# Three attentions of a two-block model: score products over 128 rows instead of 128, 64 and 96

## The chip, the cores and the metric

The kernel runs on one core of a Trainium2 chip. The time is the device time of one execution in microseconds (us), the median of the runs of the same kernel. The engines of the core are TensorE (PE in the rows, its weight loads PEld), VectorE (DVE), ScalarE (ACT), GpSimd (POOL) and SyncE (SP), whose queue issues nearly all DMAs of this kernel. A product on TensorE takes two operands from on-chip memory (SBUF): one is loaded as weights, the other streams through, and both lie with the summed index on the partitions, which are called rows here. The result goes to a bank of PSUM, where several products can be added up.

## The reference

The reference computes, for one sequence of 512 tokens with 1024 features, two blocks in a row. The first has two layers: attention over chunks with a relative bias, then a feed forward with a causal convolution; latent attention, then the same feed forward. The second has a gated feed forward, a mixer (differential attention and a matrix memory side by side), and a gated feed forward. The three attentions are what is touched. Cut to their score products:

```python
# first layer, 16 heads of 64 (chunk_rel_attention)
s = jnp.einsum('bqhd,bkhd->bhqk', qc, kc).astype(jnp.float32) * scale + bias[None]
...
# second layer, 16 heads, 64 features and 32 rotary ones (mla_attention)
s = (jnp.einsum('bqhd,bkhd->bhqk', qn, k_nope).astype(jnp.float32)
     + jnp.einsum('bqhd,bkd->bhqk', qr, k_rope).astype(jnp.float32)) * scale
...
# second block, 8 heads of two parts of 64 (diff_attention)
s = jnp.einsum('bqhcd,bkhcd->bchqk', qi, k,
               preferred_element_type=jnp.float32) * scale
```

Each is followed by a mask, a softmax over the keys and the product with the values; the differential attention subtracts the second part's probabilities from the first's with a learnt weight before that.

## The kernel before, in words

Activations lie transposed: features on the 128 partitions, the 512 tokens as columns. Every matrix operand is kept as two numbers of TensorE's fp32r type, an upper part (the value rounded) and a lower part (what is left); a product of two such operands is three products on TensorE, upper by upper, upper by lower, lower by upper (`mm3`, L325 to L329). The lower by lower product is left out there.

A head has 64 features, so one operand of 128 rows can hold an upper part in one half and a lower part in the other. `stacked` (L521) makes that from the 128 rows of a pair of heads, rows 0 to 63 of the even head and 64 to 127 of the odd one. For the queries, operand e holds the upper part in rows 64 e on and the lower part in the other rows. For the keys, operand e holds the upper part in both halves. A third tile, `low`, holds the lower parts of both heads. The moves between halves of the partitions are DMAs, two for queries and two for keys, 64 rows by 512 columns each, issued by SP. `stacked_scores` (L536) then makes the scores of a query tile of 128 with the keys up to its end (128, 256, 384 or 512 columns) of two products: queries by doubled keys over 128 rows (upper by upper and lower by upper at once, L540), then the 64 rows of the upper queries by the 64 rows of the lower keys (L541). In the latent attention a third product on the same bank adds the rotary part (L903): 32 features, stacked in 96 rows as upper, lower, upper of the queries (`qr`) against upper, upper, lower of the keys (`kr`).

`heads` (L481) runs over the heads and, for each, over four query tiles: scores, softmax on VectorE and ScalarE (`softmax`, L471, with a bias tile `b` or a mask), then, two tiles behind, the transposes of the probabilities (`transpose`, L505) and after the fourth the product with the values (`values`, L513). The score banks `ps_s` are two. The weights are streamed: `wload` (L304) loads a tile `wr` and splits it into `wh` on ScalarE and `wl` on VectorE.

The three attentions differ in how far ahead keys and queries are made. In the first layer `project(p)` (L687) makes a pair's queries and keys while the odd head of the pair before it runs. In the latent attention (L866ff) a pair is made when the even head of the pair before it begins. In the differential attention (`project(hd)`, L1247) the two parts of one head take the places of the two heads of a pair, and a head is made when the one before it begins. In the first two, a pair's output goes to memory (`pair_out`) and all outputs are brought back after the heads by `pairs_back` (L557) into two buffers of the tag `tn`, which norms use for their temporaries too; the product with the output weights follows (`branch_out`, L726).

A tile scheduler sets the order of each engine's instructions: it takes the program in the order of the code and the readiness of tiles, and lets products of the next projection fill places in which TensorE would wait for the softmax. A tile of a tag waits until the oldest of the tag's buffers is free. SP's queue is worked off in order, and a DMA that has to wait holds what stands behind it.

## Time and profile before

| | us |
| --- | --- |
| times of three runs | 2762.89, 2767.37, 2770.97 |
| median | 2767.37 |
| span of the profiled execution | 2771.6 |
| TensorE busy | 2659.2 (96%) |
| TensorE's weight loads | 2129.6 (77%) |
| VectorE busy | 1759.9 (63%) |
| ScalarE busy | 1205.0 (43%) |
| GpSimd busy | 91.8 (3%) |

The profile is of one execution, whose span is 4.2 us over the median of the timed runs. Busy shares are means over stages with different limits, so the stages have to be read one by one. The score products of the first layer run from 90 to 252 us of the span, those of the latent attention from 770 to 905, those of the differential attention from 1762 to 1944. In the rows, matmuls overlap, since the next begins while the last one's results still drain: the length of one product is no measure of its pace, the distance of two starts is. L540 is line 540 of the kernel before; an entry such as `ps_s<-k,q` names the tile written and the tiles read, and `64*128 64x512` is a weight of 64 rows by 128 columns and a moving operand of 64 rows by 512 columns.

### The profile page before, as it was taken

To read this page: it belongs to the slowest core of one execution; us is meant where nothing else is said; L and a number is where in the kernel's file an instruction comes from. 1 tells how busy PE (TensorE), PEld (TensorE's weight loads), DVE (VectorE), ACT (ScalarE), POOL (GpSimd) and SP (SyncE) were. 2 spreads that over 40 slices of the span, in tenths; PEclk is the share of its full clock that TensorE was granted. 3 is DMA by queue.
4 is the path that set the end of the run, shared out by engine and by line. 5 is a ranking of instruction groups with operands and counts; after the bars stand their busy time and mean duration, and the time that the engine had idled before them with its cause. 6 is when DMAs were issued, how large, how long until landed. Compare 5 with 4: busy or idle time off the path is not lost.

```text
span 2771.6 us, 33871 instructions
## 1 busy us (share of the span) xinstructions
PE 2659.2 (96%) x12306; PEld 2129.6 (77%) x12306; DVE 1759.9 (63%) x3349; ACT 1205.0 (43%) x2100; POOL 91.8 (3%) x138
## 2 busy tenths in 40 slices
PE   7999899999899999999899999999999999999997
PEld 5777778788677778878788888777777777788886
DVE  7777896866778896966733335788456456533334
ACT  5565532334567442324522223566446334422222
POOL 1000200000000100000100001000000000100000
PEclk9999999999899999999999999999999999999999
DMA  8664476652143475753133332322247754233331
GB/s 271 188 184 144 145 248 204 223 173 79 43 106 111 139 229 187 252 176 120 54 99 93 98 113 80 92 75 78 72 149 258 239 186 133 77 95 95 99 107 46
DMA packets 138092, 385.24 MB, mean 139 GB/s; under 512 B 22322, under 2 KB 26546, under 8 KB 137924
## 3 DMA queue, kind: packets, MB, share of 16 engines
q1 hardware_dynamic: 137924, 383.06, 43.6%
q8 instruction: 98, 1.61, 0.2%
q14 instruction: 70, 0.57, 0.1%
HBM read 341.05 MB, written 26.21 MB: 133 GB/s over the span
## 4 chain that ended last, share of the span: by engine, by line
PE 33%; issue 13%; DVE 2%; DMA 1%; ACT 1%; POOL 1%; SPq 0%; DVEq 0%; ACTq 0%; POOLq 0%
PE ps_g L329 9%; PE ps_g L327 9%; PE ps_g L328 9%; PE ps_s L541 1%; DMA stg<-xc 1%; PE ps_t L327 1%; PE ps_t L328 1%; PE ps_t L329 1%; PE ps_s L540 0%; PE ps_o L367 0%; POOL ul L400 0%; PE ps_t L509 0%; POOL acc L361 0%; DMA mv<-mv 0%; DVE tn L393 0%
## 5 line engine op out<-in xcount | busy, mean ns | idle before, releaser
L327 PE MATMUL ps_g<-uh,wh 128*128 128x512 f32 (+1 forms) x2244 | 866.2, 389 | 30.7 <-ACT uh L340 11.7
L328 PE MATMUL ps_g<-ul,wh 128*128 128x512 f32 (+1 forms) x2244 | 875.7, 391 | 15.4 <-POOL ul L400 11.9
L329 PE MATMUL ps_g<-uh,wl 128*128 128x512 f32 (+1 forms) x2244 | 868.3, 388 | 1.1 <-DVE wl L311 1.1
L310 ACT CAST wh<-wr 128x1024 fp32r<-128x1024 f32 (+4 forms) x406 | 411.6, 1015 | 990.3 <-PE ps_g L328 730.6
L311 DVE TENSOR_TENSOR wl<-wr,wh 128x1024 fp32r<-128x1024 f32 (+4 forms) x406 | 479.1, 1181 | 284.7 <-ACT wh L310 270.4
L327 PEld LDWEIGHTS ps_g<-uh,wh 128*128 128x128 f32 x2244 | 425.3, 191 | 128.5 <-ACT uh L340 14.3
L328 PEld LDWEIGHTS ps_g<-ul,wh 128*128 128x128 f32 x2244 | 428.3, 191 | 111.5 <-POOL ul L400 20.3
L329 PEld LDWEIGHTS ps_g<-uh,wl 128*128 128x128 f32 x2244 | 428.7, 191 | 89.0 <-DVE wl L311 3.8
L461 DVE CUSTOM_DVE_ANT_0 wr<-wr,cact 128x1024 f32<-128x1024 f32 x184 | 225.8, 1232 | 73.0 <-DMA wr<-mod 72.9
L327 PE MATMUL ps_g<-hidh,wh 128*128 128x512 f32 x640 | 252.9, 395 | 7.8 <-ACT hidh L340 7.8
L329 PE MATMUL ps_g<-hidh,wl 128*128 128x512 f32 x640 | 253.0, 395 | 0.9 <-DVE wl L311 0.9
L328 PE MATMUL ps_g<-hidl,wh 128*128 128x512 f32 x640 | 252.9, 395 | 0.0
L327 PEld LDWEIGHTS ps_g<-hidh,wh 128*128 128x128 f32 x640 | 120.4, 188 | 37.9 <-ACT hidh L340 9.5
L329 PEld LDWEIGHTS ps_g<-hidh,wl 128*128 128x128 f32 x640 | 120.7, 189 | 29.7 <-DVE wl L311 1.3
L328 PEld LDWEIGHTS ps_g<-hidl,wh 128*128 128x128 f32 x640 | 120.7, 189 | 29.1 <-DVE hidl L341 0.6
L444 DVE SCALAR_TENSOR_TENSOR h<-ps_g,mods,h 128x512 f32<-128x512 f32 (+1 forms) x112 | 72.8, 652 | 94.1 <-PE ps_g L329 93.5
L444 DVE SCALAR_TENSOR_TENSOR h<-ps_g,hg,h 128x512 f32<-128x512 f32 (+1 forms) x64 | 43.6, 682 | 134.4 <-PE ps_g L329 134.2
L477 ACT ACTIVATE p<-p,st 128x128 f32<-128x128 f32 (+1 forms) x192 | 107.2, 560 | 30.2 <-DVE st L476 29.2
L929 DVE TENSOR_TENSOR cv<-ps_g,cv 128x512 f32<-128x512 f32 x44 | 30.4, 691 | 137.9 <-PE ps_g L329 137.2
L361 POOL TENSOR_TENSOR acc<-acc,sq 128x256 f32<-128x256 f32 x42 | 35.9, 855 | 2049.0 <-ACT sq L360 1365.7
L340 ACT CAST hidh<-cv 128x512 fp32r<-128x512 f32 x88 | 54.6, 621 | 93.8 <-DVE cv L756 93.8
L340 ACT CAST pth<-ps_t 128x128 fp32r<-128x128 f32 (+3 forms) x160 | 65.7, 424 | 53.7 <-PE ps_t L509 52.5
(362 smaller groups left out, 3607.7 us busy)
## 6 DMA issues: line engine op xcount, KB each, us to landing
wr<-mod SPq DMA_DIRECT2D x184, 512.0 KB, 4.2
wr<-fin SPq DMA_DIRECT2D x88, 512.0 KB, 4.4
wr<-fout SPq DMA_DIRECT2D x40, 512.0 KB, 3.9
wr<-w1g SPq DMA_DIRECT2D x22, 512.0 KB, 3.6
wr<-w1u SPq DMA_DIRECT2D x22, 512.0 KB, 3.6
wr<-w2g SPq DMA_DIRECT2D x22, 512.0 KB, 3.5
wr<-w2u SPq DMA_DIRECT2D x22, 512.0 KB, 3.5
wr<-w1d SPq DMA_DIRECT2D x20, 512.0 KB, 3.6
```

The source lines that it names most:

```text
L310: nc.scalar.copy(h[:, :n], r[:, :n])
L311: nc.vector.tensor_tensor(l[:, :n], r[:, :n], h[:, :n].bitcast(F32), ALU.subtract)
L327: mm(ps, wh, xh, start=start, stop=False)
L328: mm(ps, wh, xl, start=False, stop=False)
L329: mm(ps, wl, xh, start=False, stop=stop)
L340: self.nc.scalar.copy(h, src)
L361: (eng or nc.vector).tensor_tensor(acc[:, cs], acc[:, cs], s[:, cs], ALU.add)
L444: self.nc.vector.scalar_tensor_tensor(self.h[j][:, cs], ps, g, self.h[j][:, cs], ALU.mult, ALU.add)
L461: nc.vector.tensor_tensor_reduce(w, w, cact, 1.0, 0.0, ALU.mult, ALU.add, accum_out=self.mods[:, j:j + 1])
L477: nc.scalar.activation(p[:, :n], p[:, :n], AF.Exp, bias=st[:, 0:1], scale=-1.0, accum_out=st[:, 1:2])
L541: nc.tensor.matmul(s, q[rs, qs], low[rs, ks], start=False, stop=stop)
L929: nc.vector.tensor_tensor(t, pss[1], t, ALU.mult)
```

## The change

The keys' lower parts are doubled like their upper parts. A fourth tile `low1` (tag `tn`, two buffers) holds the odd head's lower parts in both halves; the third tile, once its upper rows have been moved to `low1`, gets the even head's lower parts in both. `stacked_scores` then uses all 128 rows for the second product as well: queries with upper and lower parts by the lower parts of the keys, so the lower by lower product is now computed too. The keys need five moves instead of two; the last one, `low[b]` from `low[a]`, overwrites rows that the second and the third read. In the latent attention the rotary queries are stacked in four blocks of 32 rows (upper, lower, upper, lower) with four moves a group instead of three, and the rotary keys fill 128 rows. The diff, without the removal of comments:

```diff
     def stacked(self, src, tiles, keys, scale=1.0):
         nc = self.nc
-        x, y, low = tiles
+        x, y, low = tiles[:3]
         a, b = slice(0, 64), slice(64, 128)
         nc.scalar.mul(x, src, scale)
         nc.vector.scalar_tensor_tensor(low, src, scale, x.bitcast(F32), ALU.mult, ALU.subtract)
         nc.scalar.mul(y[b], src[b], scale)
         move = lambda o, i: nc.sync.dma_start(o.bitcast(F32), i.bitcast(F32))
-        move(y[a], (x if keys else low)[b])
-        move(x[b], (x if keys else low)[a])
+        if keys:
+            low1 = tiles[3]
+            move(x[b], x[a])
+            move(low1[b], low[b])
+            move(low1[a], low[b])
+            move(y[a], y[b])
+            move(low[b], low[a])
+        else:
+            move(y[a], low[b])
+            move(x[b], low[a])

-    def stacked_scores(self, s, q, k, low, e, i, stop=True):
+    def stacked_scores(self, s, q, k, low, i, stop=True):
         nc = self.nc
-        rs, qs, ks = slice(64 * e, 64 * e + 64), slice(i * P, i * P + P), slice(0, i * P + P)
+        qs, ks = slice(i * P, i * P + P), slice(0, i * P + P)
         nc.tensor.matmul(s, q[:, qs], k[:, ks], start=True, stop=False)
-        nc.tensor.matmul(s, q[rs, qs], low[rs, ks], start=False, stop=stop)
+        nc.tensor.matmul(s, q[:, qs], low[:, ks], start=False, stop=stop)
...
                 k = [pa.tile([P, T], F32R, tag="k", bufs=6, name="k") for _ in range(3)]
+                k.append(self.tmp(dt=F32R, tag="tn", bufs=2))
...
-                    self.stacked_scores(s, q[e], k[e], k[2], e, i)
+                    self.stacked_scores(s, q[e], k[e], k[2 + e], i)
...
-            nc.scalar.copy(kr[0:96], t[0:96])
-            nc.vector.tensor_tensor(kr[64:96], t[64:96], kr[64:96].bitcast(F32), ALU.subtract)
+            nc.scalar.copy(kr, t)
+            nc.vector.tensor_tensor(kr[64:128], t[64:128], kr[64:128].bitcast(F32), ALU.subtract)
...
-                        for q, x in enumerate((h, l, h)):
+                        for q, x in enumerate((h, l, h, l)):
...
                 kn = [pm.tile([P, T], F32R, tag="k", bufs=6, name="kn") for _ in range(3)]
+                kn.append(self.tmp(dt=F32R, tag="tn", bufs=2))
...
-                    self.stacked_scores(s, qn[e], kn[e], kn[2], e, i, False)
-                    nc.tensor.matmul(s, qr[e][0:96, qs], kr[0:96, :n], start=False, stop=True)
+                    self.stacked_scores(s, qn[e], kn[e], kn[2 + e], i, False)
+                    nc.tensor.matmul(s, qr[e][:, qs], kr[:, :n], start=False, stop=True)
...
                 qk = [pd.tile([P, T], F32R, tag="qk", bufs=10, name="qk") for _ in range(5)]
+                qk.append(self.tmp(dt=F32R, tag="tn", bufs=2))
...
-                        self.stacked_scores(s, qk[c], qk[2 + c], qk[4], c, i)
+                        self.stacked_scores(s, qk[c], qk[2 + c], qk[4 + c], i)
```

The scheduler moves instructions with it. In the three listings before and after, numbers behind names tell buffers of one name apart.

TensorE, first layer, where the fifth head (the even head of the third pair) begins, before: `ps_s` are score banks, `k` and `q` keys and queries, `ps_g` the next pair's projection from the weights `wh` and `wl`, `ps_t` transposes of the probabilities `p`.

```order
L540 MATMUL ps_s_1416<-k_1253,q_1251 128x128
L541 MATMUL ps_s_1416<-k_1255,q_1251 128x128
L540 MATMUL ps_s_1431<-k_1253,q_1251 128x256
L541 MATMUL ps_s_1431<-k_1255,q_1251 128x256
L329 MATMUL ps_g_1512<-uh_122,wl_1296 128x512
L327 MATMUL ps_g_1512<-uh_124,wh_1295 128x512
L509 MATMUL ps_t_1425<-ident_67,p_1388 128x128 x3
L328 MATMUL ps_g_1512<-ul_125,wh_1295 128x512
```

And after, at the same place (between the two pieces, 10 more products of `ps_g` and 7 transposes):

```order
L509 MATMUL ps_t_1422<-ident_67,p_1373 128x128 x2
L549 MATMUL ps_s_1432<-k_1265,q_1263 128x128
L549 MATMUL ps_s_1447<-k_1265,q_1263 128x256
L327 MATMUL ps_g_1529<-uh_124,wh_1308 128x512
L328 MATMUL ps_g_1529<-ul_125,wh_1308 128x512
...
L328 MATMUL ps_g_1529<-ul_133,wh_1308 128x512
L329 MATMUL ps_g_1529<-uh_132,wl_1309 128x512
L327 MATMUL ps_o_1463<-pth_1352,vsh_1091 64x512
L327 MATMUL ps_g_1566<-uh_118,wh_1525 128x512
L550 MATMUL ps_s_1432<-k_1267,q_1263 128x128
L550 MATMUL ps_s_1447<-k_1267,q_1263 128x256
```

Before, the second score product stood right behind the first; after, the first products of both query tiles come ahead, then products of the next projection, and the second products of both tiles follow these.

SP's queue, first layer, the moves of the same pair's keys, with what each waits for in brackets, before: `b` is a bias tile, `wr` a weight or modulation tile, `tn<-oa1` a load of `pairs_back`.

```order
L532 DMA q_1251<-sq_1287 64x512 [waits DMAHW4_49,Activation_49]
L562 DMA tn_2630<-oa1_607 128x512 [waits DMAHW5_49,DMAHW1_49]
L532 DMA k_1254<-k_1253 64x512 [waits DMAHW6_49,Activation_49]
L460 DMA wr_1966<-mod 128x1024 [waits DMAHW7_49,DVE_49]
L532 DMA k_1253<-k_1253 64x512 [waits DMAHW6_49,DMAHW0_49,DVE_49]
L702 DMA b_1583<-bias 128x512 [waits DVE_49,Pool_49]
```

And after:

```order
L533 DMA k_1265<-k_1265 64x512 [waits DMAHW7_49,DVE_49]
L533 DMA tn_1268<-k_1267 64x512 [waits DMAHW0_49]
L533 DMA tn_1268<-k_1267 64x512 [waits DMAHW1_49]
L533 DMA k_1266<-k_1266 64x512 [waits DMAHW2_49,Activation_49]
L712 DMA b_1603<-bias 128x512 [waits DMAHW3_49,DVE_49,Pool_49]
L307 DMA wr_2031<-wqk 128x1024 [waits DMAHW4_49,DVE_49]
L533 DMA k_1267<-k_1267 64x512 [waits DMAHW5_49,DMAHW1_49,DMAHW0_49]
L307 DMA wr_2068<-wqk 128x1024 [waits DMAHW6_49,DVE_49]
```

The two moves of the keys became five, the last waits for the landings of the two into `tn` (DMAHW0 and DMAHW1), a weight load stands right behind it, and the load `tn<-oa1` has gone from this place to behind the heads.

TensorE, first layer, the last but two of the heads, query tiles two and three, before: `ps_g_2676` and `ps_g_2702` are products with the output weights, `ps_o` those with the values.

```order
L540 MATMUL ps_s_2347<-k_2004,q_2002 128x256
L541 MATMUL ps_s_2347<-k_2005,q_2002 128x256
L509 MATMUL ps_t_2356<-ident_67,p_2241 128x128 x4
L540 MATMUL ps_s_2378<-k_2004,q_2002 128x384
L541 MATMUL ps_s_2378<-k_2005,q_2002 128x384
L327 MATMUL ps_g_2676<-uh_2626,wh_2672 128x512
L328 MATMUL ps_g_2676<-ul_2627,wh_2672 128x512
L329 MATMUL ps_g_2676<-uh_2626,wl_2673 128x512
L327 MATMUL ps_o_2363<-pth_2164,vsh_2079 64x512
L327 MATMUL ps_g_2676<-uh_2632,wh_2672 128x512
L328 MATMUL ps_g_2676<-ul_2633,wh_2672 128x512
```

And after:

```order
L549 MATMUL ps_s_2379<-k_2028,q_2026 128x256
L550 MATMUL ps_s_2379<-tn_2030,q_2026 128x256
L509 MATMUL ps_t_2388<-ident_67,p_2269 128x128 x4
L549 MATMUL ps_s_2410<-k_2028,q_2026 128x384
L550 MATMUL ps_s_2410<-tn_2030,q_2026 128x384
L327 MATMUL ps_o_2395<-pth_2192,vsh_2107 64x512
L509 MATMUL ps_t_2419<-ident_67,p_2368 128x128
L549 MATMUL ps_s_2423<-k_2028,q_2026 128x512
```

The products with the output weights between the score products have gone from here; they stand behind the heads now.

## Rows read from the trace of the kernel before

**Rows 1.** The page: span, and each engine's busy time, share and instructions.
```profile
span 2771.6 us, 33871 instructions
...
PE 2659.2 (96%) x12306; PEld 2129.6 (77%) x12306; DVE 1759.9 (63%) x3349; ACT 1205.0 (43%) x2100; POOL 91.8 (3%) x138
```

**Rows 2.** Table by stretch: length, PE, PEld, DVE, ACT, POOL, PEclk, DMA share, GB/s.
```profile
90.00:262.00 172.00, 169.36 (x819) 122.91 (x820) 136.98 (x422) 108.83 (x263) 2.44 (x14) 0.99 0.56 169
770.00:906.00 136.00, 134.43 (x678) 96.06 (x677) 108.89 (x360) 96.26 (x251) 0.00 (x0) 0.95 0.38 105
1762.00:1945.00 183.00, 182.48 (x928) 141.59 (x927) 146.00 (x412) 121.61 (x280) 0.00 (x0) 1.00 0.28 78
```

**Rows 3.** TensorE's waits, 75 to 262 us: total, times, longest.
```profile
PE ps_s L540 <- DMA k<-k: 3.6, 1, 3.6
PE ps_s L540 <- DVE st L476: 1.5, 2, 1.2
```

**Rows 4.** TensorE's timeline in stage B: start, length, instruction.
```profile
809.01 0.39 PE L540 MATMUL ps_s<-kn,qn 128*128 128x512 f32 x1
809.33 0.49 PE L541 MATMUL ps_s<-kn,qn 64*128 64x512 f32 x1
809.75 0.50 PE L903 MATMUL ps_s<-kr,qr 96*128 96x512 f32 x1
810.09 0.39 PE L328 MATMUL ps_o<-ptl,vs 128*64 128x512 f32 x1
810.32 0.39 PE L329 MATMUL ps_o<-pth,vs 128*64 128x512 f32 x1
810.54 0.34 PE L327 MATMUL ps_o<-pth,vs 128*64 128x384 f32 x1
```

**Rows 5.** TensorE's timeline in stage A.
```profile
170.27 0.40 PE L540 MATMUL ps_s<-k,q 128*128 128x512 f32 x1
170.60 0.50 PE L541 MATMUL ps_s<-k,q 64*128 64x512 f32 x1
171.03 0.50 PE L329 MATMUL ps_g<-uh,wl 128*128 128x512 f32 x1
171.37 0.39 PE L328 MATMUL ps_o<-ptl,vsh 128*64 128x512 f32 x1
```

**Rows 6.** TensorE's timeline in stage C.
```profile
1821.92 0.50 PE L541 MATMUL ps_s<-qk 64*128 64x512 f32 x1
1822.35 0.50 PE L540 MATMUL ps_s<-qk 128*128 128x512 f32 x1
1822.78 0.50 PE L541 MATMUL ps_s<-qk 64*128 64x512 f32 x1
```

**Rows 7.** TensorE's timeline in the mixer, behind the differential attention.
```profile
2187.76 1.77 PE L1128 MATMUL ps_t<-slr 10*128 10x512 f32 x4
2189.46 0.50 PE L327 MATMUL ps_g<-uh,wh 128*128 128x512 f32 x1
2189.80 0.39 PE L328 MATMUL ps_g<-ul,wh 128*128 128x512 f32 x1
```

**Rows 8.** Instructions on ps_s: count, min/median/max ns, first and last start, forms.
```profile
L541 PE MATMUL ps_s<-k,q x64: 323/409/676, 90.5 to 251.5; 64*128 64x128 f32 x16, 64*128 64x256 f32 x16, 64*128 64x384 f32 x16, 64*128 64x512 f32 x16
```

**Rows 9.** DMA issues: count, KB each, median us from issue to landing.
```profile
k<-k SPq DMA_DIRECT2D x16, 128.0 KB, 4.1
...
kn<-kn SPq DMA_DIRECT2D x16, 128.0 KB, 2.3
...
qk<-qk SPq DMA_DIRECT2D x16, 128.0 KB, 2.2
```

**Rows 10.** Table by stretch, in the middle of stage B.
```profile
870.00:900.00 30.00, 30.00 (x157) 20.76 (x155) 25.82 (x88) 23.04 (x62) 0.00 (x0) 1.00 0.46 130
```

**Rows 11.** Table by stretch, at the first heads of stage B.
```profile
770.80:774.20 3.40, 3.07 (x11) 1.64 (x11) 2.52 (x10) 1.65 (x6) 0.00 (x0) 1.00 0.52 119
774.20:787.90 13.70, 13.24 (x45) 9.08 (x43) 8.09 (x31) 6.63 (x20) 0.00 (x0) 0.50 0.41 108
```

## The prediction

> **What bounds the kernel now.** The page comes first: over the span of 2771.6 us TensorE is busy 96% [rows 1]. A busy share alone doesn't prove a bound, so the second view is the table by stretch, cut at the three stages that the change touches: the relative-bias attention of the first layer (stage A), the latent attention (stage B) and the differential attention (stage C). TensorE is busy 169 of 172, 134 of 136 and 182 of 183 us there; VectorE 137, 109 and 146 [rows 2]. So TensorE sets the pace in all three, but VectorE is only 14 to 20% behind it. The third view is the waits of TensorE inside stage A: the longest is a single one of 3.6 us, on a key's DMA, the next are two of together 1.5 us, on VectorE [rows 3].
>
> The fourth view is the timeline, read from start to start, because the modelled ends overlap. A stream of 128-row products of 512 columns goes at 0.23 and 0.22 us each (mean 0.225), at the end of [rows 4]. A score tile doesn't: in stage B the first product is followed after 0.32 us, the 64-row product after 0.42, the 96-row one after 0.34, and only then is the pace back. In stage A it is 0.33, 0.43 and 0.34 [rows 5]. The columns are the same, so around each 64-row product TensorE loses 0.10 before it, 0.20 on it and 0.11 on the next, 0.40 us in all (taken between 0.405 and 0.425 of the two places, and rounded down). In stage C, where 64-row and 128-row products alternate, each start comes 0.43 after the last: twice 0.20 per pair, the same sum [rows 6]. The 96-row product that follows a 64-row one shows only the return that a 128-row product shows too, so 96 rows stand with 128. That it is the row count and not these tiles is seen far away: in the mixer four products over 10 rows start 0.425 apart (1.70 by 4), and the 128-row product behind them takes 0.34 [rows 7].
>
> **The change, part by part.** *Row counts.* The second score product goes from 64 to 128 rows, the rotary one from 96 to 128. Columns, counts and order of accumulation stay, so a product at the normal pace costs the same, and what goes is the loss of 0.40 us. There are 64 such products in each stage, 192 in all (16 for each number of columns; [rows 8] has stage A's, and B's and C's lines read the same but for the operands). I counted what follows them on TensorE: a product in 43, 58 and 42 cases, a transpose in 21, 6 and 22. Behind a transpose the return can't be told apart from the transpose's own step, so there only 0.10 + 0.19 = 0.29 counts. Stage A: 43 x 0.40 + 21 x 0.29 = 23.3 us. Stage B: 58 x 0.40 + 6 x 0.29 = 24.9. Stage C: 42 x 0.40 + 22 x 0.29 = 23.2. The ceiling is 71.4 us, if nothing else becomes late.
>
> The Trainium skill has a rule that speaks against this: by "TensorE: Matmul & The Clock Gate", section "The mechanism" of Part 3 and the list behind it, a weight load runs beside products in flight only when it targets other row groups, and a load over all 128 rows would therefore stand in the open. The trace doesn't bear it out: the 128-row stream of [rows 4] keeps 0.225 us a product with a load for each. By the rule the sum would lose about a load on each of 192 products; it is the last rival below.
>
> *DMAs of the keys.* Five moves of 64 rows instead of two for each of 24 pairs or heads, 72 more of 128 KB, and 16 more rotary moves of 64 KB. The volume, some 10 MB, is small beside queues that are 0.56, 0.38 and 0.28 busy in these stages [rows 2]. What matters is the chain. The last move overwrites rows that two others read, so SP issues it only when both have landed, and the lower parts of an even head come two landings after VectorE's subtraction instead of at once. A landing of such a move took 4.1 us in stage A, 2.3 in B and 2.2 in C [rows 9]. In B and C the keys are projected two heads or one long head ahead, 17 and 23 us (136 us by 16 heads, 183 by 8), which hides two landings: nothing. In stage A they are projected one head ahead, about 11 us. There the new order puts products and short transposes between the first and the second score product of an even head: 20, 8, 17, 17, 17, 18, 8 and 3 products for the eight pairs, at 0.225 us. So 4.5 and 3.8 us cover the added landing of 4.1 nearly, 1.8, 1.8 and 0.7 don't: 2.3 + 2.3 + 3.4 = 8 us. Were the landing 2.3 as in stage B, 2.6 us would be left. Bounds are 0 (SP gets there early) and 8 x 4.1; I take 5, between the two counts.
>
> *End of stage A.* The first two of the loads that bring the heads' outputs back used free buffers early; now both buffers of that tag hold keys of the last pairs. So heads 13 and 14 lose their filler, products of the output weights: none now, 13 before. 13 x 0.225 = 3 us of work moves behind the heads, and TensorE may stand still for as long. Bounds: nothing, and 3 plus an uncovered landing of 4.1 at the last pair. I take 3.
>
> *VectorE as the next bound.* This is where part of the gain goes. In the middle of stage B, VectorE is busy 25.8 us of 30 while TensorE never pauses [rows 10]. TensorE would need 30 less 3.5 heads of 4 x 0.39 us, 24.5: less than VectorE. The shortest that the 30 us can become is 25.8 (VectorE without a gap, 14% less, 19 us of the stage's 136), the longest 30. VectorE waits in order for ScalarE and TensorE in the softmax, so I take the middle, a share of 0.93: 27.8 us, 7.5% of 136, **10 us** instead of 24.9. In stage C, 146 us of VectorE in 183 - 23 = 160 is 0.91, still under 0.93: TensorE stays the bound, and I keep **22** of 23.2. In stage A, 137 in 172 - 23 = 149 is 0.92: it holds too, less the 5 and 3 from above, **15**.
>
> *Clock.* In stage B the granted clock was at half, 0.50 (1.2 GHz), for 13.7 us, after 3.4 us in which TensorE ran 11 products, busy 3.07, at 1.00 (2.4 GHz) [rows 11]. If that stretch goes, up to half of its 13.7 us, 6.9, come back; if heads without filler bring another like it, as much is lost. I take zero; both ends are in the range.
>
> **Sum**: 15 + 10 + 22 = 47 us, from the profiled span of 2771.6 to 2724.6. The median of the timed runs, 2767.4, is 4.2 us below that span, so the time is 2767.4 - 47 = 2720.
>
> **Rivals.** (1) *TensorE stays the bound everywhere.* VectorE fits in, the chain is covered. For it: VectorE isn't full in any of the three. 2767.4 - 71.4 = 2696. (2) *VectorE and the key chain take more.* Stage B gains nothing (the long end above), stage A has four of its eight pairs uncovered by 4.1 us (16 us) and keeps 7, C keeps 16: 2744. (3) *Slower: SP's queue.* SP issues in order, and behind the fifth move stand the next weight loads. If its wait reaches TensorE each time, 8 x 4.1 + 8 x 2.3 + 8 x 2.2 = 69 us are lost, and 5 of that is already in my sum: 2720 + 64 = 2784. For it: the one long wait of TensorE in stage A was already on a key's DMA [rows 3]. Against it: none of its longest waits there was for a weight. It decides from the point where a load is issued less than a landing, cast and subtraction ahead of its use; at three quarters of the 64 the gain is gone. (4) *No change.* The loss belongs to a second product on the same bank, not to row counts: 2767. Against it: a third product on that bank goes at the normal return, and the 10-row products show the same loss elsewhere. (5) *Loads in the open.* With a load and its product one after the other, each of the 192 products costs a load more. For its price, the 64-row product's excess of 0.20 us is the nearest row [rows 5]: 192 x 0.2 = 38 us, so 2758. Beside it: this is what the clock-gate page's rule would do.
>
> **Chances.** Forecast 0.53, (1) 0.14, (2) 0.16, (3) 0.08, (4) 0.06, (5) 0.03. The range runs from the ceiling to just past case (2), 2697 to 2748, and leaves out (3), (4), (5) and a little of (1). About 0.3% (8 us) is what a measurement of this kernel can tell from no change, since its three times lie 0.3% apart. Faster: the forecast, (1), (2) and half of (5), 0.85. Same: (4) and the rest of (5), 0.07. Slower: 0.08.
>
> **What would show it.** In the changed profile, second score products that start 0.22 to 0.23 us after the first at 512 columns prove the row-count step; still 0.32 and 0.42 would prove (4). Stages of 157, 126 and 161 us instead of 172, 136 and 183 prove the sum; VectorE above 9 of 10 us in stage B with TensorE pausing ahead of score products proves the second bound. A wait of the second score product on a key's DMA, once per even head in stage A, shows the chain, and waits of TensorE for wh or wl show (3). I am wrong altogether if the pace of 128-row score products isn't that of the stream in [rows 4].

## The result and the profile after

The changed kernel takes 2730.07 us (median of 4 runs, 2726.74 to 2732.18), the kernel before 2769.17 beside it (4 runs). The ratio is 0.9857, 95% interval 0.9840 to 0.9873: 39 us less, where the prediction said 47 (2720, range 2697 to 2748). The sign and most of the size came out; the three stages that make up the sum did not, and of the reasons one fell and one holds only in part.

The page of the changed kernel, its span and the busy time of its engines, answers to [rows 1]:

```profile
span 2730.3 us, 34039 instructions
...
PE 2598.0 (95%) x12306; PEld 2113.4 (77%) x12306; DVE 1756.8 (64%) x3349; ACT 1201.7 (44%) x2100; POOL 92.4 (3%) x138
```

TensorE's busy time falls by 61 us, the span by 41: 20 us of the gain have become idle time. Where, the table by stretch tells. It is cut here from the first to the last score product of each stage (A, B, C as in the prediction), first for the kernel before, then for the changed one. The columns are those of [rows 2].

```profile
90.30:251.50 161.20, 158.84 (x760) 114.76 (x760) 128.03 (x405) 101.24 (x248) 2.44 (x14) 0.99 0.57 173
770.10:905.00 134.90, 133.33 (x672) 95.27 (x671) 107.79 (x357) 95.45 (x249) 0.00 (x0) 0.95 0.38 105
1762.40:1943.50 181.10, 180.58 (x920) 140.18 (x918) 144.57 (x406) 120.33 (x277) 0.00 (x0) 1.00 0.28 78
```

```profile
88.50:243.40 154.90, 143.98 (x761) 112.24 (x762) 128.15 (x402) 98.87 (x245) 2.51 (x14) 0.98 0.65 196
762.50:880.60 118.10, 111.14 (x663) 88.69 (x664) 101.84 (x349) 91.69 (x244) 0.00 (x0) 0.99 0.55 144
1739.50:1904.20 164.70, 160.98 (x920) 137.20 (x919) 141.90 (x404) 117.86 (x275) 0.00 (x0) 1.00 0.38 103
```

A gains 6.3 us (15 were predicted), B 16.8 (10), C 16.4 (22): 39.5 in all. The rest of the program is within 2 us. The idle time of TensorE, length less busy, goes from 2.4 to 10.9 us in A, from 1.6 to 7.0 in B, from 0.5 to 3.7 in C.

The timeline of the changed kernel around a score tile in stage B answers to [rows 4] (start, length, instruction):

```profile
793.48 0.45 PE L549 MATMUL ps_s<-kn,qn 128*128 128x512 f32 x1
793.76 0.40 PE L550 MATMUL ps_s<-kn,qn 128*128 128x512 f32 x1
794.00 0.40 PE L914 MATMUL ps_s<-kr,qr 128*128 128x512 f32 x1
794.23 0.40 PE L328 MATMUL ps_o<-ptl,vs 128*64 128x512 f32 x1
794.47 0.39 PE L329 MATMUL ps_o<-pth,vs 128*64 128x512 f32 x1
```

From the second product to the third 0.24 us instead of 0.42, from the third on 0.23 instead of 0.34: the pace of the stream, as the first step of the prediction said. What is left is 0.28 ahead of the second product.

TensorE's waits in stage A of the changed kernel answer to [rows 3] (total, times, longest):

```profile
PE ps_s L549 <- DMA k<-k: 6.1, 4, 3.2
PE ps_o L327 <- ACT pth L340: 2.7, 7, 1.0
PE ps_s L550 <- DMA k<-k: 2.5, 3, 1.0
PE ps_t L509 <- DVE ptl L341: 0.8, 1, 0.8
PE ps_t L509 <- DVE st L478: 0.7, 2, 0.4
```

Read alone, this list names the key moves, 8.6 us on `k<-k`, and that was my first reading of stage A. Of these, 3.2 us lie ahead of the stage's first score product, where the kernel before waits 3.6 us [rows 3]; 5.4 us lie in the stage. The experiments bore the reading out only in part.

### The profile page after: what moved, and what is told of

Read it like the earlier page. It is cut to its first block, busy times and chain, and to the rows that moved or that the text cites. A ratio compares the mean times of both kernels' runs of the same rounds, so it can differ in the third digit from the quotient of the medians.

```text
span 2730.3 us, 34039 instructions
## 1 busy us (share of the span) xinstructions
PE 2598.0 (95%) x12306; PEld 2113.4 (77%) x12306; DVE 1756.8 (64%) x3349; ACT 1201.7 (44%) x2100; POOL 92.4 (3%) x138
## 4 chain that ended last, share of the span: by engine, by line
PE 33%; issue 13%; DVE 2%; ACT 1%; DMA 1%; POOL 1%; SPq 0%; DVEq 0%; ACTq 0%; POOLq 0%
PE ps_g L327 9%; PE ps_g L328 9%; PE ps_g L329 9%; PE ps_t L328 1%; PE ps_t L327 1%; PE ps_t L329 1%; PE ps_o L367 0%; PE ps_s L549 0%; POOL ul L400 0%; PE ps_s L550 0%; DMA stg<-xc 0%; POOL acc L361 0%; PE ps_t L1139 0%; DVE h L280 0%; PE ps_o L327 0%
## 5 line engine op out<-in xcount | busy, mean ns | idle before, releaser
L397 ACT ACTIVATE uh<-tn,mods 128x256 fp32r<-128x256 f32 (+1 forms) x120 | 60.4, 519 | 53.5 <-DVE tn L393 52.7
```

What stands on the lines that cost most here:

```text
L397: nc.scalar.activation(h[:, cs], t, AF.Identity, bias=sh)
```

## The experiments

Theory M was the prediction's: row counts bring the gain, key moves and lost filler take some of it in stage A, VectorE in stage B. After the first group it had to be changed; theory L (the latency of the softmax chain) was set against it, and it holds only in part too. One table first, of each kernel's three stages, cut as above. The column "half" is the time in A, in us, at a granted clock of 0.50 (1.2 GHz). In the kernel before, products over 128 rows and 512 columns start 0.43 us apart there and 0.23 us apart at 1.00. So one us of it does half the work, and lengths of A differ by some us for that alone, by most in x7. "At an equal clock" below means a length less half of that time. Stage A of x3 has the program of the changed kernel's, and at an equal clock the two traces still differ by 2.6 us: smaller differences of A between kernels with key moves say nothing. x1, x8 and x12, without the moves, agree within 1 us.

| kernel | ratio to before (95%) | A | idle in A | half in A | B | C |
| --- | --- | --- | --- | --- | --- | --- |
| before | 1 | 161.2 | 2.4 | 3.4 | 134.9 | 181.1 |
| changed | 0.9857 (0.9840 to 0.9873) | 154.9 | 10.9 | 6.6 | 118.1 | 164.7 |
| x1, rows only | 0.9829 (0.9805 to 0.9853) | 153.8 | 11.4 | 10.2 | 118.5 | 164.2 |
| x2, moves only | 1.0016 (1.0002 to 1.0031) | 165.1 | 3.5 | 10.2 | 135.3 | 181.1 |
| x3, rotary 96 rows | 0.9843 (0.9820 to 0.9866) | 155.9 | 12.6 | 3.4 | 116.5 | 164.7 |
| x4, other tag | 0.9849 (0.9826 to 0.9873) | 155.3 | 10.6 | 3.4 | 118.5 | 164.8 |
| x5, x1 and lag 3 | 0.9804 (0.9789 to 0.9819) | 144.3 | 2.7 | 3.4 | 117.6 | 164.2 |
| x6, x1 and less VectorE | 0.9830 (0.9809 to 0.9852) | 152.6 | 11.0 | 10.2 | 118.9 | 164.2 |
| x7, before and less VectorE | 0.9984 (0.9971 to 0.9997) | 168.4 | 2.9 | 23.9 | 133.8 | 181.1 |
| x8, x1 with 96, 32, 80 rows | (one run) | 149.7 | 9.6 | 3.1 | 135.2 | 164.4 |
| x9, changed and lag 3 | 0.9861 (0.9837 to 0.9885) | 147.9 | 8.0 | 0 | 118.3 | 164.8 |
| x10, before and lag 3 | 0.9999 (0.9983 to 1.0015) | 159.0 | 0 | 6.2 | 135.8 | 181.1 |
| x11, x5 with three score banks | 1.0028 (1.0012 to 1.0045) | 143.8 | 2.1 | 5.6 | 120.9 | 164.8 |
| x12, x1 and mixer rows | 0.9801 (0.9772 to 0.9830) | 149.5 | 9.8 | 3.0 | 118.5 | 164.3 |

### Row counts without the moves (x1)

The tile `low` already holds lower parts in all its rows, in each half those of one head. Taking all 128 rows of it adds the lower query parts of head e by the lower key parts of the other head: as small as the lower by lower product that the kernel leaves out anyway. So the row count can be had alone, on one line:

```diff
-        nc.tensor.matmul(s, q[rs, qs], low[rs, ks], start=False, stop=stop)
+        nc.tensor.matmul(s, q[:, qs], low[:, ks], start=False, stop=stop)
```

> The kernel before with one line changed: the second score product takes all 128 rows of the queries and of the unchanged tile low, whose other half holds the other head's lower parts (what they add is lower by lower, as small as what is left out anyway). No added move, no tile from tn, rotary at 96 rows. Theory M (the row count is the gain; the key moves and the lost filler at the end of the first attention took 8 us of it): first attention 21 to 23 us shorter than before where the changed kernel is 6 to 8 shorter, the others as in the changed kernel within 2 us, in all 2712 to 2718 us. Rival S (the softmax chain on VectorE and ScalarE is the bound in all three once the loss is gone, moves cost nothing): 2728 to 2732, as the changed kernel. Rival D (the doubled keys themselves bring the gain): 2767.

Measured: ratio 0.9829, the gain of the changed kernel without any added DMA or tile. In all three stages TensorE has the order of the kernel before, product for product. This shows that the row count is the cause, and that the doubled keys aren't (D). But stage A is 153.8, not 138 to 140 as M said, and the total of 2726.7 us lies nearest to rival S's. The waits of TensorE in A:

```profile
PE ps_s L540 <- DMA k<-k: 4.9, 2, 3.4
PE ps_t L509 <- DVE p L711: 4.9, 4, 2.0
PE ps_s L540 <- DVE st L476: 2.4, 2, 1.8
PE ps_o L327 <- ACT pth L340: 1.7, 6, 0.3
```

Without the added moves there are fewer waits on `k<-k` (3.4 of the 4.9 us lie ahead of the stage), and new ones on the softmax (`p`, `st`) stand in their place; the idle time is the same 11 us. The moves alone can't be the cause of the loss in A.

### The moves without the row counts (x2)

```diff
-        nc.tensor.matmul(s, q[:, qs], low[:, ks], start=False, stop=stop)
+        rs = slice(64 * e, 64 * e + 64)
+        nc.tensor.matmul(s, q[rs, qs], low[rs, ks], start=False, stop=stop)
```

> The changed kernel with all its moves and tiles, but the second score product back at 64 rows (the rotary one stays at 128). Theory M: all the cost and no gain: first attention 6 to 10 us longer than in the kernel before, latent and differential within 2 us, in all 2775 to 2781 us. Rival S (moves cost nothing): 2769 within 3. Rival Q (SP's queue is held up in all three stages by the fifth move): 2790 and more, with longer latent and differential stages too.

Measured: ratio 1.0016, some 4 us, against the 6 to 12 of M. Stage A is 3.9 us longer than before, of which its longer time at half clock (10.2 us against 3.4) makes about 3.4; B and C don't move. So behind 64-row products 72 key moves and 16 rotary moves cost little, and rival Q (SP's queue held up) is out: neither of the lengths that it names grew by more than 0.4 us. The trace has one cost of the moves outside the three stages. Ahead of stage B's first score product TensorE waits for a move of the queries, here and with the same line in the changed kernel:

```profile
PE ps_s L549 <- DMA qn<-sq: 3.2, 1, 3.2
```

The kernel before and x1 don't wait there; x3, with three rotary moves a group, waits 0.8 us.

### The rotary product at 96 rows (x3)

```diff
-            nc.scalar.copy(kr, t)
+            nc.scalar.copy(kr[0:96], t[0:96])
...
-                    nc.tensor.matmul(s, qr[e][:, qs], kr[:, :n], start=False, stop=True)
+                    nc.tensor.matmul(s, qr[e][0:96, qs], kr[0:96, :n], start=False, stop=True)
...
-                        for q, x in enumerate((h, l, h, l)):
+                        for q, x in enumerate((h, l, h)):
```

> The changed kernel with the rotary part as before: three blocks, 96 rows, three moves a group. Theory M (96 rows run at the pace of 128): 2730 within 3 us. Rival (any count under 128 loses): 64 products would lose 0.4 us each, some 25 us, less what VectorE hides, 2745 to 2755.

Measured: ratio 0.9843, B 116.5. 96 rows cost what 128 cost; the fourth block of the rotary part brings nothing.

### The fourth key tile out of the tag `tn` (x4)

```diff
-                k.append(self.tmp(dt=F32R, tag="tn", bufs=2))
+                k.append(self.tmp(dt=F32R, tag="acc", bufs=3))
```

> The changed kernel, but in the first attention the fourth key tile takes a buffer of the tag acc (three buffers) instead of tn, so that the first two loads of the heads' outputs go early again and the last heads have the products of the output weights between their score products. Theory M: the last two pairs of the first attention get 3 us back, 2727 (2724 to 2729). Rival (the key chain alone costs, filler nothing): 2730 within 1.5.

Measured: ratio 0.9849 and A 155.3. A gain of 3 us is smaller than the intervals, so the times can't tell M from its rival. The trace can in part: stage A holds 776 products instead of 761 for 0.4 us more, and from its end to the first score product of B it takes 514.6 us instead of 519.1, with 23.9 us at half clock in both. So in these two traces the filler brings 4.1 us, 2.6 at an equal clock: about the term of 3 us, but behind the stage. TensorE's idle time in A doesn't change by it (10.6 and 10.9 us).

### One tile more of lag (x5), and less work for VectorE (x6, x7)

If not the moves, what does TensorE wait for in A? Either VectorE has no time left, or one pass through the softmax takes too long for the two tiles of lag. x5 gives it a third:

```diff
-            self.heads(pa, 16, begin)
+            self.heads(pa, 16, begin, 3)
...
-            self.heads(pm, 16, begin)
+            self.heads(pm, 16, begin, 3)
```

> The kernel x1 (row counts alone) with the transposes of the first and the latent attention three query tiles behind the softmax instead of two. In x1 TensorE idles 11 us among the score products of the first attention (2 before) and 8 in the latent one (2 before). Theory L (the latency of one softmax chain, VectorE, ScalarE, VectorE, is what TensorE now waits for): with one tile more of slack most of it goes, 10 to 15 us less than x1, 2712 to 2717. Theory V (VectorE and ScalarE have no more room, so slack doesn't help): as x1, 2727 within 5. Rival K (the waits are for the keys of the next pair, by DMA): as x1 as well, with the waits of x1 on k still there.

x6 and x7 take work off VectorE instead, with and without the row counts, in A and B (left out is the division of the probabilities by their sum):

```diff
-                    nc.vector.tensor_scalar(pr[:, :n], pr[:, :n], st[:, 2:3], None, ALU.mult)
```

> x1 without the products of the probabilities by 1/sum on VectorE in the first and the latent attention (left out: the normalization of the softmax there; 64 instructions, some 24 us of VectorE in each of the two). Theories V and L: idle of TensorE among the score products falls from 11 and 8 us to 3 to 5 in each, the first attention from 154 to 146 to 149 us, the latent from 118 to 112 to 115, in all about 2715. Rival K (keys by DMA): first attention 152 to 154 still, total 2722 or more.

> The kernel before (64 rows) without the same VectorE instructions (left out: the normalization in the first and the latent attention). If VectorE was no bound before, as the prediction says, next to nothing comes of it: TensorE idles 2.4 and 1.6 us there, so 0 to 4 us less than before. Rival (VectorE was already part of the bound): the same 10 to 12 us less as x6 has below x1.

Measured, x5: stage A in the table by stretch, and its waits on TensorE:

```profile
91.10:235.40 144.30, 141.60 (x760) 112.13 (x761) 126.05 (x400) 98.81 (x246) 2.41 (x14) 0.99 0.63 191
```

```profile
PE ps_s L540 <- DMA k<-k: 3.8, 2, 3.3
PE ps_s L540 <- DVE st L476: 1.1, 4, 0.3
PE ps_o L327 <- ACT pth L340: 0.8, 2, 0.6
```

The waits on `p` are gone, idle time is back at 2.7 us, and A is 9.5 us shorter than in x1, with the same VectorE work. Some 3.4 of the 9.5 are the shorter time at half clock; against x8, whose stage A has the same order on TensorE as x1 and 3.1 us at half clock, 5.4 remain:

```profile
90.20:239.90 149.70, 140.12 (x761) 111.39 (x761) 126.15 (x402) 100.25 (x248) 2.16 (x14) 0.99 0.61 185
```

With a lag of two tiles and no key moves TensorE idles 9.6 to 11.4 us in A (x1, x8, x12), with three 2.1 and 2.7 (x11, x5). So rival K falls: the idle time goes without a change to the DMAs. Theory L had 10 to 15 us less than x1 in all; by the ratios it is some 7, and their intervals overlap. B does not move (117.6).

Measured, x6: stages A and B in the table by stretch:

```profile
89.90:242.50 152.60, 141.63 (x754) 112.63 (x754) 108.99 (x339) 99.31 (x246) 2.03 (x14) 0.97 0.59 180
755.90:874.80 118.90, 109.75 (x667) 87.60 (x667) 88.62 (x297) 94.14 (x250) 0.00 (x0) 1.00 0.43 119
```

VectorE has 17 us less to do in each (108.99 against x1's 126.53, 88.62 against 105.18), and the stages are 1.2 shorter and 0.4 longer than in x1. VectorE's capacity bounds neither. In x7 the same edit brings 0.16% of the whole; its A is longer, with 23.9 us at half clock, and its B 1.1 us shorter. But theory L missed here as well as V: the edit takes a link out of the softmax chain, both had the idle time fall to 3 to 5 us, and it is 11.0 and 9.2. Of the expectations only rival K's numbers came out, and K is what x5 refutes. The longest waits in A are now on the score banks:

```profile
PE ps_s L540 <- DVE st L476: 6.0, 7, 2.5
```

x5 changes TensorE's order in A and B, and so does x6. What is shown is that VectorE's load isn't the limit and that one tile more of lag, with the order that comes of it, takes the idle time of A away. That the length of the softmax chain is the reason is argued, and x6 speaks against a simple form of it. The control for the lag is x10.

### The lag in the kernel before (x10) and in the changed one (x9)

The same edit of `heads` as in x5, on the other two kernels.

> The kernel before with the same three tiles of lag. Theory L (the latency was hidden as long as the 64-row products were slow): TensorE idles only 2.4 us in the first attention there, so 0 to 3 us, 2769 to 2776 against 2774 of before. Rival (the lag is a gain of its own, whatever the rows): 8 to 10 us less, as x5 against x1.

> The changed kernel, doubled keys and all moves, with the transposes of the first and the latent attention three query tiles behind the softmax as in x5. Theory L (in the changed kernel too it is the softmax's latency that took the gain of the first attention, not the key moves): first attention from 155 to 145 to 148 us, in all 2718 to 2723, within 4 us of x5. Rival C (the chain of key moves holds it): 152 to 155, in all 2727 to 2731, with TensorE's waits on k as they are.

Measured, x10: ratio 0.9999. In the whole time the lag is worth nothing that can be measured behind 64-row products; stage A of x10 has no idle time left:

```profile
90.60:249.60 159.00, 159.00 (x760) 115.76 (x760) 128.20 (x401) 100.51 (x247) 2.28 (x14) 0.98 0.55 173
```

But at an equal clock (6.2 us at half against 3.4) stage A is 3.6 us shorter than before; from x8 to x5 it is some 5.5. So in A most of what the lag gives, it gives behind 64-row products too; only the idle time that it removes grows with the row counts, from 2.4 us to between 7 and 9. x10 and x5 have one order on TensorE, as the kernel before and x1 have. At an equal clock the row counts take 13.3 us off A with the lag of three and 10.8 to 11.5 with the lag of two (x1, x8, x12): some 2 us of their gain, not 5 to 9, is what the lag of two had withheld.

Measured, x9: stage A is 147.9, as theory L said, but still 8.0 us idle:

```profile
PE ps_s L549 <- DMA k<-k: 3.7, 4, 2.9
PE ps_s L549 <- DMA b<-bias: 2.3, 1, 2.3
PE ps_t L509 <- DVE ptl L341: 1.8, 2, 1.3
```

Part of what waits there is a DMA again (2.9 of the 3.7 us on `k` lie ahead of the stage), a bias that stands behind four of the key moves in SP's queue among it. At an equal clock x9's A is some 5 us longer than x5's (147.9 with none at half clock, 144.3 with 3.4 us). And the whole kernel's ratio, 0.9861, shows no gain over the changed kernel's, where rival C put it: the profiled executions lie 5.7 us apart, the medians only 2.0. The profiled execution of x9 has its 7 us less in A, of which 3.3 are the clock, and 3 us more between A and B (522.2 instead of 519.1). So with the longer lag the moves still cost A some 5 us, with the shorter one taking them out (x1) leaves the idle time as it is: only without both does it go. How much of the chain's cost comes out once the lag is longer is left open by this run; that x5, without the chain, is faster than the changed kernel (0.9804 against 0.9857, intervals apart) is measured.

### Other row counts (x8)

```diff
-        nc.tensor.matmul(s, q[:, qs], low[:, ks], start=False, stop=stop)
+        nc.tensor.matmul(s, q[rs, qs], low[rs, ks], start=False, stop=stop)
```

with `rs` as rows 0 to 95 in A, 32 rows in B, rows 0 to 79 in C.

> x1 with other row counts of the second score product: 96 rows in the first attention, 32 in the latent, 80 in the differential one (left out: part of the lower key parts of some heads). Theory of a threshold above 64: pace of 96 rows as 128 (0.23 us to the next product at 512 columns), of 32 as 64 (0.42); 80 open. Rival (the loss grows with the rows that are missing): 96 loses 0.1 us, 80 some 0.15, 32 0.3 per product. So stage lengths: 154, 135 and 164 or 181 by the threshold; 160, 143 and 175 by the rival.

Measured: B is 135.2, the length before; C is 164.4, as with 128 rows. The timeline, 32 rows in B and 80 in C:

```profile
793.21 0.39 PE L540 MATMUL ps_s<-kn,qn 128*128 128x512 f32 x1
793.53 0.49 PE L541 MATMUL ps_s<-kn,qn 32*128 32x512 f32 x1
793.95 0.50 PE L903 MATMUL ps_s<-kr,qr 96*128 96x512 f32 x1
794.29 0.39 PE L328 MATMUL ps_o<-ptl,vs 128*64 128x512 f32 x1
...
1782.63 0.41 PE L541 MATMUL ps_s<-qk 80*128 80x512 f32 x1
1782.87 0.40 PE L540 MATMUL ps_s<-qk 128*128 128x512 f32 x1
1783.10 0.40 PE L541 MATMUL ps_s<-qk 80*128 80x512 f32 x1
```

32 rows have the steps of 64 rows in [rows 4], 0.32, 0.42 and 0.34; 80 rows have 0.24 and 0.23. The loss doesn't grow with the missing rows: it is there in full at 64 and 32, and not at 80, 96 and 128.

### Three score banks (x11)

```diff
-        return self.ps.tile([P, n], F32, tag=tag, bufs={"g": 3, "s": 2, "t": 2, "o": 1}[tag], name="ps_" + tag)
+        return self.ps.tile([P, n], F32, tag=tag, bufs={"g": 2, "s": 3, "t": 2, "o": 1}[tag], name="ps_" + tag)
...
-            banks = [self.pg(tag=c) for c in "gggsstto"]
+            banks = [self.pg(tag=c) for c in "ggssstto"]
...
-            em = self.pg()
+            em = self.pg(tag="s")
```

> x5 with three score banks instead of two and two projection banks instead of three (one product of the matrix memory moves to a score bank for that). In x5 TensorE still idles some 6 us in the latent attention, the larger part until VectorE has read a score bank. If the two banks are what holds it, the idle falls to 2 to 3 us there and the latent attention from 118 to 113 to 115; what two projection banks cost elsewhere is open (0 to 30 us in all). Rival (the chain itself is late, not the bank): 117 to 118 as in x5.

Measured: B 120.9, three us longer than in x5 (1.7 of them are the clock, 3.4 us at half against none), and 50 us more in the rest, where projections lost a bank. In B the wait on a score bank falls (3.2 to 2.0 us), those on the transposes' results rise:

```profile
PE ps_t L509 <- DVE ptl L341: 2.1, 7, 0.5
PE ps_o L327 <- ACT pth L340: 2.0, 5, 0.7
PE ps_s L540 <- DVE st L476: 2.0, 3, 1.4
```

So a third score bank, at the price of a projection bank, doesn't shorten B; its idle time is 7.4 us, against 6.2 in x5. What the 6 to 9 us of idle time there wait for in the end was not found: VectorE's load (x6) and the lag (x5) are out, and the score banks as far as this exchange of banks can tell.

### The 10-row products of the mixer (x12)

```diff
-                nc.tensor.matmul(ar[:, :n], slr[0][hr, js], slr[1][hr, P * j:], start=True, stop=True)
+                nc.tensor.matmul(ar[:, :n], slr[0][:, js], slr[1][:, P * j:], start=True, stop=True)
```

> x1 with the products over 10 rows in the mixer (L1128, plain fp32) taken over all 128 rows (the computation is changed there: the sums run over all four heads and the unused rows). The prediction read their pace as the same loss by rows. If so, at 512 columns the step between the two passes of one product falls from 0.43 to 0.23 us, the first product behind them from 0.34 to 0.23 and the step into them from 0.31 to 0.23; 16 of them, 6 to 10 us in all if nothing else holds it. Rival (the plain fp32 type is slow whatever the rows): steps as before.

Measured, the timeline of x12 at the place that answers to [rows 7]:

```profile
2130.17 0.39 PE L329 MATMUL ps_g<-uh,wl 128*128 128x512 f32 x1
2130.40 1.67 PE L1128 MATMUL ps_t<-slr 128*128 128x512 f32 x4
2131.61 0.69 PE L327 MATMUL ps_g<-uh,wh 128*128 128x512 f32 x1
2132.13 0.40 PE L328 MATMUL ps_g<-ul,wh 128*128 128x512 f32 x1
```

And of x1, with 10 rows:

```profile
2141.44 0.39 PE L329 MATMUL ps_g<-uh,wl 128*128 128x512 f32 x1
2141.76 1.77 PE L1128 MATMUL ps_t<-slr 10*128 10x512 f32 x4
2143.46 0.50 PE L327 MATMUL ps_g<-uh,wh 128*128 128x512 f32 x1
2143.80 0.39 PE L328 MATMUL ps_g<-ul,wh 128*128 128x512 f32 x1
```

The four are two products of two passes each, one of 512 and one of 384 columns. From the product ahead of the four to the second behind them it is 1.96 us instead of 2.36: 0.40 less for the whole group. Into it, the step falls from 0.32 to 0.23. But the pace within stays: single records of the trace have the steps behind passes over 512 columns at 0.43 us with 128 rows, at 0.53 (the first) and 0.43 with 10. So 0.43 there is the pace of plain fp32, as the rival said, and the loss by rows is 0.40 for one visit of four passes, not for each product. From the first to the last of these products x12 takes 71.0 us, x1 75.6, and 1.7 of the difference is the clock (3.4 us at half in x1, none in x12): less than the 6 to 10 that were expected. The whole of x12 is some 0.3% below x1, the intervals overlap, and part of that is the granted clock behind A to C.

## Why the prediction was right or wrong, point by point

**The row-count step was right in kind.** x1 brings the gain with this alone, x8 takes it away in B with 32 rows, and x2 has the moves without it. Rivals 4 (the bank) and 5 (loads in the open) fall with them: 128-row score products go at 0.23 us with a load for each. So the rule of the Trainium skill's "TensorE: Matmul & The Clock Gate", Part 3, "The mechanism", that a load runs beside products in flight only when it targets other row groups, did not show as a cost here. One proof was misread: the four starts "0.425 apart" in the mixer [rows 7] are a mean over passes of 512 and 384 columns (0.53, 0.43, 0.32 and 0.41 us), and x12 has 0.43 and 0.32 with 128 rows too. Only the steps into and out of such a visit show the row count.

**Its size was too large.** The ceiling of 71.4 us took 0.40 from tiles of 512 columns for all four widths. Added up over all starts at an equal clock, the steps into and out of the second products (those at which the product begins or ends) fell by 16.6, 16.2 and 18.2 us from the kernel before to x1, which has the same order on TensorE: 51 us, 0.27 per product. Two things were missed. Narrow tiles didn't gain as much: products of 128 columns on 128 columns of weights start 0.11 us apart in x1's mixer:

```profile
2148.24 0.27 PE L329 MATMUL ps_s<-mq,mk 128*128 128x128 f32 x1
2148.35 0.28 PE L327 MATMUL ps_s<-mq,mk 128*128 128x128 f32 x1
2148.46 0.28 PE L328 MATMUL ps_s<-mq,mk 128*128 128x128 f32 x1
```

Before, the step behind a second product of 128 columns was 0.25 us, in x1 it is 0.11; so it gives back 0.14, not 0.20. And a first product right behind a transpose keeps some 0.08 us of its own, with 128 rows too. The return of 0.11 on the next product, which the sum has 143 times, doesn't come out as a sum of its own in the other steps: from the kernel before to x5 they differ by less than 1 us in A and rise by 1 in C, where new waits on the softmax lie among them.

**Stage A, 15 predicted, 6.3 measured.** Of the miss of 8.7 us, 6.7 are the size of the row-count step (16.6 of 23.3) and 1.6 the clock (6.6 us at half instead of 3.4). The new idle time, 8.5 us, is close to the 8 that were priced for key moves and filler, and that is luck: the cover in A had no term for the softmax at a lag of two tiles, and without the moves the idle time is the same (x1). It goes only without the moves and with a longer lag (x5); with the longer lag alone 8.0 us stay (x9). The filler's 3 us stand behind the stage (x4). The profile of before could have warned: behind the key's DMA, A's list of waits already had the softmax in it, 1.5 us on `st` [rows 3].

**Stage B, 10 predicted, 16.8 measured.** 13.7 us at half clock became 3.4 (0.95 and 0.99 of the whole stretch in the tables above), worth about 5 us; the prediction named this and took zero. It goes with the row counts: the traces with 64 or 32 rows in B have 13.7 or 16.9 us at half clock there, those with 128 rows 0 to 6.8. The other 11.7 are close to the 10, but not for the reason given: VectorE as the bound at a share of 0.93 is refuted by x6, and its share in the changed kernel is 0.86 (101.84 of 118.10). The "14 to 20%" that VectorE was said to be behind are 19 to 20% by [rows 2]; the 14% are those of [rows 10]. The step was 16.2 instead of the 24.9 of the ceiling, and new idle time, 5.4 us, took a third of it. Most of TensorE's waits there are on the softmax chain; which of its links sets this is open. That the key moves in B cost nothing held inside the stage; ahead of it they left the wait of 3.2 us that x2 shows.

**Stage C, 22 predicted, 16.4 measured.** The stage held, as said, and C differs by under 1 us in all kernels with over 64 rows. The miss is the size of the row-count step (18.2 of 23.2) and 3.2 us of new idle time.

**Rivals and sum.** The three misses are -8.7, +6.8 and -5.6 us, -7.5 in all; the total was nearer than its parts by luck, since the clock in B, taken at zero, made up for a good part of the step that came out too small everywhere. Rival 3 (SP's queue) is out: no wait of TensorE on `wh` or `wl` in stage A, and x2 nearly free. Of what would show the steps, the pace was right in A (median step from first to second product at 512 columns 0.23 us) and nearly in C (0.26); in B it is 0.30, where transposes stand close by.

**A version faster than both** is x5: one line changed in `stacked_scores`, two in the calls of `heads`, no added DMA. Its ratio is 0.9804 (0.9789 to 0.9819), 2720.5 us where the kernel before takes 2776.3 beside it.

## What to carry to other kernels

Look at the starts, not at the busy share: TensorE was 96% busy before and still lost some 50 us to products over 64 rows or less. Before operands are copied to fill the rows, see whether the rows that lie there already hold something harmless. And when a stage's bound gets faster, ask not only which engine is next in busy time but what each tile has to wait for: in stage A the engine with the next highest share was no limit, 17 us less of its work left the idle time as it was, and one tile more of lag took 7 to 9 us of it away. Compare such stages at an equal clock and with the control, or the clock and the lag's own gain are put down to the change.

## What was not expected of the hardware

The loss is a step, not a slope: 10 (in plain fp32), 32 and 64 rows have it, 80, 96 and 128 do not. The mixer's four passes over 10 rows lose 0.40 us together, as much as a single 64-row product of 512 columns: it is paid on the way in and on the way out. Whether 64-row products standing next to one another would share it too was not tried. The Trainium skill's "TensorEngine Tiling (Array Packing)", section "Tiling Modes", has a rule that fits, which the prediction did not use: the array can be split by rows into tiles of 64 or 32 (part "Available Configurations"), and changing the mode drains the engine (part "Key Properties"). The runs agree with it in where the loss sits (ahead of, on and behind a visit) and at which counts (none at 80 and 96, which no tile of 64 rows holds); that a drain is what happens there, they don't show.
